# Values of heads 2 and 3 as 512-column products, with their weights split ahead and the first two token tiles run in turns

## The chip, the cores and the metric

The kernel runs on one core of one Trainium2 chip. The metric is the device time of one execution in microseconds (us); the median of several runs counts. Shares and instruction times come from one profiled execution.

## The reference

One layer of an encoder over 1024 tokens of width 1024, all in float32. What matters here is the input projection and the gated linear attention that reads it:

```python
h = rmsnorm(x, norm_mix)
proj = h @ w_in                      # -> q (512), k (512), v (1024), r (1024), decay, pool input, gates
qh, kh: 4 heads of 128 columns       # q scaled by 128 ** -0.5
vh:     4 heads of 256 columns
o = gla_chunked(q, k, v, decay_fwd) + flip(gla_chunked(flipped, decay_bwd))
o = o * rsqrt(mean(o * o)) * gla_norm * silu(r)
```

In `gla_chunked` each chunk of tokens takes scores of q and k, products of the scores with the values, and a state that is carried from chunk to chunk (keys times values, with a decay), forwards and backwards. Then come two branch projections with gates, an output projection, a feed-forward layer and a last norm.

## The kernel before

**Products.** Every float32 operand is split in two float32r parts, high and low (`split_to`: a cast on ACT, a subtraction on DVE or, for most weights, on POOL). A product is three matmuls (`mm3`, L276, through `products` on L274): high x high, high x low, low x high. The normalized and transposed activations lie in `hT`, 8 feature tiles of 128 by 1024 tokens, in SBUF.

**Projections of the heads.** q and k of a head (`project_qk`, L730) are feature-major: for each half of the tokens, 8 steps of `mm3` with 512 columns. Values are token-major: the stationary operand is a tile of 128 tokens, the moving one the weights. For heads 0 and 1 the weights of both heads (512 columns) are kept split in SBUF from the beginning, and `pair_products` (L493) makes both heads' values at once, 512 columns to a matmul. For heads 2 and 3, each in its turn, `values` (L422) makes one token tile: 8 steps of `mm3` with 256 columns, then `split_to` into `vh` and `vl`.

**Weights.** `order` (L238) lists the weight blocks to be loaded; `fetch` issues the next load (`raw` tiles, four buffers, 256 KB each), `prepare` puts the splits of a block in the list `pending`, and `take` hands out the next block and prepares the one after. The split parts lie in `wh` and `wl`, six buffers each. All loads and most stores go through SyncE's queue, in order.

**Order of the work.** Instructions are issued in the order in which the program names them; each engine works through its own in order. `mm3` ends with `pump(columns / 512)` (L161), which counts in steps of one 512-column product: every 2 such steps it runs one entry of `pending`; then, when `pending` is empty, at most one step of `aside` (jobs that form sums of later weights on POOL and store them, `beside` on L677 with `branch_jobs` on L618); then the steps of `side`. A step there is a generator that yields how many units it lets pass. `attention(h, q, k)` (L740) is such a generator: decay terms on ACT and DVE (`exponentials`, `apply_decay`), transposed keys (`kp`, `kt`), then the wait until head h's values are there, the backward states (`kv`, `st`, `sb`, `so`), scores (`sc`, `p`) and the forward pass with outputs (`op`, `o`). Generators run one after another, so head h's attention starts when head h-1's has ended. It runs beside the projections of later heads. `normalize` of a finished head is run by the next head's attention, which also issues the store of its output (`o_out`, `flush`).

**Buffers.** 39 slots of 4 KB a partition hold activations, values, keys, states, sums. PSUM has three banks for projections (`ps_mm`) and five for attention and transposes (`ps_g`). A new tile waits for the last reader of the one that it replaces.

After the heads come eight r products (L1123), beside which head 3's attention ends and the sums of the activations for the next stage are made (`feature_jobs`, L648; tiles `hs`, `trh`, `trl`), and then the gate stage, which multiplies with them.

Of the kernel before, what the change touches and what calls it, by code (L numbers as in the profile page):

```python
# [10 lines left out]
F32 = mybir.dt.float32  # L11
# [6 lines left out]
P = 128  # L18
# [35 lines left out]
def kernel(  # L54
# [38 lines left out]
    def name(s):  # L93
        count[0] += 1
        return f"{s}_{count[0]}"

    def slot(dtype=F32, shape=(2, HALF), s="slot"):
        return slots.tile([P, *shape], dtype, tag="slot", name=name(s))
# [10 lines left out]
    def bank(pool, s="ps"):  # L109
        return pool.tile([P, HALF], F32, tag=pool.name, name=name(s))  # L110

    def as_f32(ap):
        return ap.bitcast(F32)
# [85 lines left out]
    def split_to(hi, lo, src, eng=nc.vector):  # L199
        nc.scalar.copy(hi, src)  # L200
        eng.tensor_tensor(lo, src, as_f32(hi), op=ALU.subtract)  # L201

    def load(src, kts, c0, width):
        per = min(HALF // width, kts)
        tiles = []
        for k0 in range(0, kts, per):
            raw = wts.tile([P, per, width], F32, tag="raw", name=name("raw"), bufs=4)
            nc.sync.dma_start(
                raw[:, :, :],
                src[k0 * P : (k0 + per) * P, c0 : c0 + width].rearrange("(k p) c -> p k c", p=P),  # L210
            )
            tiles.append(raw)
        return tiles

    class Weights:


        def __init__(self, tiles):
            self.per = tiles[0].shape[1]
            self.parts = []  # L220
            self.todo = [partial(self.split, raw) for raw in tiles]
            pending.extend(self.todo)

        def split(self, raw):
            hi = wts.tile(list(raw.shape), F32R, tag="wh", name=name("wh"))[:, :, :]
            lo = wts.tile(list(raw.shape), F32R, tag="wl", name=name("wl"))[:, :, :]
            split_to(hi, lo, raw[:, :, :], nc.gpsimd if hT.tiles else nc.vector)
            self.parts.append((hi, lo))
# [8 lines left out]

    order = []  # L238
    for h in range(HEADS):
        cols_of = [(Q0 + h * DK, DK), (K0 + h * DK, DK), (V0 + h * DV, DV)]  # L240
        order += [(w_in, KT, *c) for c in cols_of[: 2 if h < 2 else 3]]
    order += [(w_in, KT, R0 + j * P, P) for j in range(KT)]
    order = iter(order)
    loaded, ready = [], []
# [6 lines left out]
    def prepare():  # L251
        if not loaded:
            fetch()
        if loaded:
            ready.append(Weights(loaded.pop(0)))

            credit[0] = -2.0

    def take(ahead=True):

        if not ready:
            prepare()
        w = ready.pop(0)
        w.finish()
        if ahead:
            prepare()
        return w
# [3 lines left out]
    def products(ps, a, b, first=True, last=True, onto=False):  # L271

        for n, (i, j) in enumerate(((0, 0), (0, 1), (1, 0))):
            nc.tensor.matmul(ps, a[i], b[j], start=first and n == 0, stop=last and n == 2, skip_group_check=onto)  # L274

    def mm3(ps, a, b, first, last, onto=False):  # L276
        products(ps, a, b, first, last, onto)
        pump(ps.shape[-1] / HALF)
# [15 lines left out]
    def tokens(pair, t):  # L294
        return tuple(p[:, (t % 4) * P : (t % 4 + 1) * P] for p in pair)
# [123 lines left out]
            norm_x(t)  # L419
            yield 2  # L420

    def values(w, v, t):  # L422
        ps = bank(ps_mm)
        for kt in range(KT):
            mm3(ps[:, :DV], tokens(hT(kt, t // 4), t), w(kt), kt == 0, kt == KT - 1)
        split_to(*(part[:, t % 4, :] for part in v[t // 4]), ps[:, :DV])

    lw = [wts.tile([P, 4, 4, 2 * RANK], F32R, tag="wh", name=name("lw")) for _ in range(2)]
    up = slot(F32R, (HEADS, 2, DK), "up")

    def low_rank_weights():
# [3 lines left out]
            nc.vector.tensor_tensor(lw[i][:, :, 3, :], raw, as_f32(lw[i][:, :, 0, :]), op=ALU.subtract)  # L438
        nc.scalar.copy(up[:, :, :, :], uraw[:, :, :, :])
        nc.vector.tensor_tensor(up[32:64], uraw[32:64], as_f32(up[32:64]), op=ALU.subtract)  # L440

    def value_slots():
        return [(slot(F32R, (4, DV), "vh"), slot(F32R, (4, DV), "vl")) for _ in range(2)]

    cols = const.tile([P, 40], F32, tag="cols", name="cols")

# [41 lines left out]
    split_pair_weight()  # L488
    for kp in range(2):
        transpose_tile(trs[kp], xn[1], 1, kp)  # L490
    pair_v = [[], []]

    def pair_products(ts, before=None):  # L493
        banks = [bank(ps_mm) for _ in ts]
        for k in range(KT):
            if before:
                before(k)
            for ps, t in zip(banks, ts):
                mm3(ps[:, :], tokens(hT(k, t // 4), t), pair_w[k], k == 0, k == KT - 1)
        for ps, t in zip(banks, ts):  # L500
            for h in range(2):
                if t // 4 == len(pair_v[h]):
                    pair_v[h].append((slot(F32R, (4, DV), "vh"), slot(F32R, (4, DV), "vl")))
            parts = [[part[:, t % 4, :] for part in v[t // 4]] for v in pair_v]
            halves = [ps[:, h * DV : (h + 1) * DV] for h in range(2)]
            for (hi, _), src in zip(parts, halves):
                nc.scalar.copy(hi, src)
            for (hi, lo), src in zip(parts, halves):
                nc.vector.tensor_tensor(lo, src, as_f32(hi), op=ALU.subtract)

    def first_steps(k):
        if k == 2:
# [204 lines left out]
    def prepare_beside(jobs, every, put=PUT, lag=1):  # L717
        aside.append([beside(chain(*jobs), every, put, lag), every])
# [8 lines left out]
    v_heads, o_heads, unscaled = {}, {}, []  # L727
    HOLD, SCORES = 4.4, 6

    def project_qk():  # L730
        q = slot(s="q")
        k = slot(s="k")
        for dst, scale in ((q, DK**-0.5), (k, 1.0)):
            w = take()
            for half in range(2):
                ps = feature_major(w, hT, half)
                nc.scalar.activation(dst[:, half, :], ps[:, :], AF.Copy, scale=scale)
        return q, k
# [220 lines left out]
    def first_qk():  # L959
        q, k = slot(s="q"), slot(s="k")  # L960
        low_rank(0)
        weights = [take()]
        for half in range(2):
            if half:
                finish_side()
                low_rank(1)
                prepare()
            for n, (dst, scale) in enumerate(((q, DK**-0.5), (k, 1.0))):
                if n == len(weights):
                    weights.append(take(ahead=False))  # L970
                ps = feature_major(weights[n], hT, half)
                nc.scalar.activation(dst[:, half, :], ps[:, :], AF.Copy, scale=scale)
        return q, k

    for h in range(HEADS):
        qk = project_qk() if h else first_qk()
        begin(attention(h, *qk))
        if h == 0:
            for ts in ((7,), (6,), (5, 4)):
                pair_products(ts)  # L980
            v_heads.update(enumerate(pair_v))
            prepare_beside(map(branch_jobs, range(4)), 5)
        if h > 1:
            v = value_slots()
            w = take()
            for t in range(NT):
                values(w, v, t)
            v_heads[h] = v

    class Unit:  # L990

# [1041 lines left out]
```

## Time and profile before

| | |
|---|---|
| time, median of 3 runs (range) | 1379.97 us (1379.44 to 1380.46) |
| the profiled execution | 1380.1 us |
| its span, first to last instruction | 1378.1 us |
| granted TensorE clock, mean | 0.999 |
| instructions | 18207, of them 6514 matmuls |
| value products of heads 2 and 3 | 384 matmuls of 256 columns, 154.3 to 264.5 us |
| head 2's projections begin | about 131 us |
| r products begin | about 269 us |

In the profile PE is TensorE's matmuls, PEld its weight loads, DVE VectorE, ACT ScalarE, POOL GpSimd, SP SyncE. A timeline row has the start and the duration in us, the engine, the line of the kernel and the operation, output and inputs by name; in brackets stands how long the engine was idle before it and what it waited for. A row of the waits has the total in us, how often, and the longest. A row of a stretch of time has its length, then the busy time of an engine in it and the count of instructions, the granted clock, the DMA share and GB/s.

### The profile page before, as it was taken

How to read it: one execution, taken by the hardware profiler on the slowest of the kernel's cores; microseconds unless marked ns; L12 is line 12 of the kernel's file. 1: busy time of each engine (PE TensorE's matmuls, PEld its weight loads, DVE VectorE, ACT ScalarE, POOL GpSimd, SP SyncE). 2: the span in 40 equal slices, each digit the busy share in tenths (PEclk: the TensorE clock that was granted, in tenths of full speed). 3: DMA queues.
4: the chain of work that ended last, by engine and by line, in shares of the span. 5: the costliest groups of instructions: out<-in, count | busy, mean ns of one | idle time of the engine just before them, and what ended most of it. 6: DMA issues, size and time to landing. Idle time of an engine off the chain costs nothing. (4 is left out here: it accounts for less than half of the span.)

```text
span 1378.1 us, 18207 instructions
## 1 busy us (share of the span) xinstructions
PE 1367.6 (99%) x6514; PEld 1147.4 (83%) x6514; DVE 839.8 (61%) x1027; ACT 642.6 (47%) x1170; POOL 750.7 (54%) x554
## 2 busy tenths in 40 slices
PE   9999999999999999999999999999999999999998
PEld 7888899988888888888888888888888888888886
DVE  6364656557745876688883955656656556343375
ACT  7375666655334445554347533333333334444353
POOL 3222617132297646668665276666666667455454
PEclk9999999999999999999999999999999999999999
DMA  6121413312478678996516355555544447985561
GB/s 226 31 62 47 147 62 125 110 48 77 138 230 278 197 229 277 371 394 216 175 61 245 115 176 176 176 176 176 165 143 139 144 136 266 385 306 186 170 214 77
DMA packets 166586, 243.60 MB, mean 177 GB/s; under 512 B 10936, under 2 KB 95968, under 8 KB 166496
## 3 DMA queue, kind: packets, MB, share of 16 engines
q1 hardware_dynamic: 166352, 242.18, 52.3%
q8 instruction: 51, 0.84, 0.3%
q14 instruction: 39, 0.32, 0.1%
q10 hardware_dynamic: 144, 0.26, 0.1%
HBM read 164.55 MB, written 77.86 MB: 176 GB/s over the span
## 5 line engine op out<-in xcount | busy, mean ns | idle before, releaser
L201 POOL TENSOR_TENSOR wl<-fs,wh 128x512 fp32r<-128x512 f32 x120 | 167.6, 1400 | 157.2 <-ACT wh L200 103.2
L274 PE MATMUL ps<-gh,wh 128*128 128x512 f32 x616 | 240.9, 391 | 0.0
L274 PE MATMUL ps<-gl,wh 128*128 128x512 f32 x616 | 240.2, 390 | 0.3 <-DVE gl L1591 0.3
L274 PE MATMUL ps<-gh,wl 128*128 128x512 f32 x616 | 240.0, 390 | 0.0
L201 POOL TENSOR_TENSOR wl<-fraw,wh 128x512 fp32r<-128x512 f32 x90 | 129.7, 1441 | 63.6 <-ACT wh L200 61.2
L274 PE MATMUL ps<-hh,wh 128*128 128x512 f32 x376 | 151.9, 404 | 0.0
L201 POOL TENSOR_TENSOR ol<-gor,oh 128x1024 fp32r<-128x1024 f32 (+1 forms) x42 | 101.7, 2425 | 85.7 <-ACT oh L200 59.6
L274 PE MATMUL ps<-hh,wl 128*128 128x512 f32 x376 | 146.9, 391 | 0.0
L274 PE MATMUL ps<-hl,wh 128*128 128x512 f32 x376 | 146.8, 390 | 0.0
L274 PEld LDWEIGHTS ps<-gl,wh 128*128 128x128 f32 x616 | 115.8, 188 | 24.1 <-DVE gl L1591 0.7
L274 PEld LDWEIGHTS ps<-gh,wh 128*128 128x128 f32 x616 | 115.8, 188 | 24.0 <-ACT hb L1610 0.3
L274 PEld LDWEIGHTS ps<-gh,wl 128*128 128x128 f32 x616 | 115.7, 188 | 24.1
L201 POOL TENSOR_TENSOR wl<-raw,wh 128x512 fp32r<-128x512 f32 x40 | 54.7, 1379 | 121.9 <-ACT wh L200 103.5
L274 PE MATMUL ps<-oh,oh 128*128 128x512 f32 x308 | 120.0, 390 | 0.0
L274 PE MATMUL ps<-oh,ol 128*128 128x512 f32 x308 | 120.0, 390 | 0.0
L274 PE MATMUL ps<-ol,oh 128*128 128x512 f32 x308 | 120.0, 389 | 0.0
L201 POOL TENSOR_TENSOR wl<-wraw,wh 128x512 fp32r<-128x512 f32 x56 | 92.2, 1675 | 44.7 <-ACT wh L200 44.5
L201 DVE TENSOR_TENSOR ol<-wor,oh 128x1024 fp32r<-128x1024 f32 (+1 forms) x42 | 62.8, 1506 | 68.1 <-ACT oh L200 55.5
L200 ACT CAST wh<-fs 128x512 fp32r<-128x512 f32 x120 | 73.8, 615 | 26.1 <-DVE fs L1010 25.1
L274 PEld LDWEIGHTS ps<-hh,wl 128*128 128x128 f32 x376 | 70.6, 188 | 15.0
L274 PEld LDWEIGHTS ps<-hl,wh 128*128 128x128 f32 x376 | 70.9, 188 | 12.9
L274 PEld LDWEIGHTS ps<-hh,wh 128*128 128x128 f32 x376 | 70.8, 188 | 12.8
(279 smaller groups left out, 3126.3 us busy)
## 6 DMA issues: line engine op xcount, KB each, us to landing
fraw<-in_w_ffn_in_dram SPq DMA_DIRECT2D x44, 512.0 KB, 7.2
gor<-g_out SPq DMA_DIRECT2D x35, 512.0 KB, 5.8
g_out<-s SPq DMA_DIRECT2D x44, 256.0 KB, 2.3
raw<-in_w_in_dram SPq DMA_DIRECT2D x40, 256.0 KB, 5.1
fraw<-in_w_in_dram SPq DMA_DIRECT2D x20, 512.0 KB, 7.1
wor<-t_out SPq DMA_DIRECT2D x20, 512.0 KB, 4.5
g_out<-g SPq DMA_DIRECT2D x33, 256.0 KB, 2.5
x<-in_x_dram SPq DMA_DIRECT2D x16, 512.0 KB, 4.5
```

What stands on the lines that cost most here:

```text
L200: nc.scalar.copy(hi, src)
L201: eng.tensor_tensor(lo, src, as_f32(hi), op=ALU.subtract)
L274: nc.tensor.matmul(ps, a[i], b[j], start=first and n == 0, stop=last and n == 2, skip_group_check=onto)
```

## The change

Values of heads 2 and 3 are made together, in the turn of head 2, by a new class `ValueWeights`. Its weights are 8 blocks of 128 features by 512 columns (both heads). It is created as head 2's q weights are taken: two loads at once, four splits put in `pending`, each split first issuing the load four further on. Two more splits are put there when head 2's k weights are taken, and the last two run when the products begin. Feature tiles 6 and 7 are split into slots, the other six into `wh` and `wl`, all six buffers of each. `products` runs token tile 7 with the six weights that come first, then tile 6 with the same six, then tile 7 with the other two, tile 6 with the other two, and tiles 5 to 0 with all eight. Tile 2 issues the load of head 3's q weights; in tile 0, after two weights, their splits are prepared. `keep_values` empties a bank: two casts on ACT, two subtractions on DVE. It is taken out of `pair_products`, which now calls it. The branch sums of `aside` are split in two batches: two jobs after head 0's values with a pace of 3.7 units instead of 5, two after the values of heads 2 and 3 with a pace of 4. `order` no longer has value blocks.

```diff
-        cols_of = [(Q0 + h * DK, DK), (K0 + h * DK, DK), (V0 + h * DV, DV)]
-        order += [(w_in, KT, *c) for c in cols_of[: 2 if h < 2 else 3]]
+        order += [(w_in, KT, c + h * DK, DK) for c in (Q0, K0)]
...
+    class ValueWeights:
+        ORDER = (0, 1, 6, 7, 2, 3, 4, 5)
+        IN_SLOTS = (6, 7)
+        def __init__(self):
+            self.raw, self.parts = [], {}
+            self.load(2)
+            self.splits(4)
+        def load(self, upto):
+            while len(self.raw) < min(upto, KT):
+                k = self.ORDER[len(self.raw)]
+                raw = wts.tile([P, HALF], F32, tag="raw", name=name("raw"), bufs=4)
+                nc.sync.dma_start(raw[:, :], w_in[k * P : (k + 1) * P, V0 + 2 * DV : V0 + 4 * DV])
+                self.raw.append(raw)
+        def split(self):
+            n = len(self.parts)
+            self.load(n + 4)
+            k = self.ORDER[n]
+            if k in self.IN_SLOTS:
+                w = slot(F32R, s="wv")
+                parts = w[:, 0, :], w[:, 1, :]
+            else:
+                parts = [wts.tile([P, HALF], F32R, tag=s, name=name(s))[:, :] for s in ("wh", "wl")]
+            split_to(*parts, self.raw[n][:, :], nc.gpsimd)
+            self.parts[k] = parts
+        def splits(self, n):
+            pending.extend([self.split] * n)
+        def products(self):
+            while pending:
+                pending.pop(0)()
+            vs, banks = ({}, {}), {}
+            self.split()
+            self.split()
+            def steps(t, ks):
+                if t not in banks:
+                    banks[t] = bank(ps_mm)
+                for k in ks:
+                    if (t, k) == (0, 6):
+                        prepare()
+                        credit[0] = 1.0
+                    at = self.ORDER.index(k)
+                    mm3(banks[t][:, :], tokens(hT(k, t // 4), t), self.parts[k], at == 0, at == KT - 1)
+                if ks[-1] == self.ORDER[-1]:
+                    keep_values(vs, t, banks[t])
+            early, late = self.ORDER[:6], self.ORDER[6:]
+            for ks in (early, late):
+                for t in (7, 6):
+                    steps(t, ks)
+            for t in reversed(range(NT - 2)):
+                if t == 2:
+                    fetch()
+                steps(t, self.ORDER)
+            return vs
...
-    def project_qk():
+    def project_qk(last=False):
...
-            w = take()
+            final = last and dst is k
+            w = take(not final)
+            if final:
+                value_weights[0].splits(2)
+            elif last:
+                value_weights.append(ValueWeights())
...
-        qk = project_qk() if h else first_qk()
+        qk = project_qk(h == 2) if h else first_qk()
...
-            prepare_beside(map(branch_jobs, range(4)), 5)
-        if h > 1:
-            v = value_slots()
-            w = take()
-            for t in range(NT):
-                values(w, v, t)
-            v_heads[h] = v
+            prepare_beside(map(branch_jobs, range(2)), 3.7)
+        if h == 2:
+            v_heads.update(zip((2, 3), value_weights.pop().products()))
+            prepare_beside(map(branch_jobs, range(2, 4)), 4)
```

More of the change, by code (lines that the diff above doesn't have):

```diff
@@ L420, in norms @@
             yield 2
[L422 to L426, printed above, removed]
     lw = [wts.tile([P, 4, 4, 2 * RANK], F32R, tag="wh", name=name("lw")) for _ in range(2)]
@@ L440, in low_rank_weights @@
         nc.vector.tensor_tensor(up[32:64], uraw[32:64], as_f32(up[32:64]), op=ALU.subtract)
-    def value_slots():
-        return [(slot(F32R, (4, DV), "vh"), slot(F32R, (4, DV), "vl")) for _ in range(2)]
     cols = const.tile([P, 40], F32, tag="cols", name="cols")
@@ L490, with keep_values @@
         transpose_tile(trs[kp], xn[1], 1, kp)
-    pair_v = [[], []]
+    pair_v = {}, {}
+    def keep_values(vs, t, ps):
+        for v in vs:
+            if t // 4 not in v:
+                v[t // 4] = slot(F32R, (4, DV), "vh"), slot(F32R, (4, DV), "vl")
+        parts = [[part[:, t % 4, :] for part in v[t // 4]] for v in vs]
+        halves = [ps[:, h * DV : (h + 1) * DV] for h in range(2)]
+        for (hi, _), src in zip(parts, halves):
+            nc.scalar.copy(hi, src)
+        for (hi, lo), src in zip(parts, halves):
+            nc.vector.tensor_tensor(lo, src, as_f32(hi), op=ALU.subtract)
     def pair_products(ts, before=None):
@@ L500, in pair_products @@
         for ps, t in zip(banks, ts):
[L501 to L509, printed above, removed]
+            keep_values(pair_v, t, ps)
     def first_steps(k):
@@ L973, in first_qk @@
         return q, k
+    value_weights = []
     for h in range(HEADS):
-        qk = project_qk() if h else first_qk()
+        qk = project_qk(h == 2) if h else first_qk()
         begin(attention(h, *qk))
```

## The prediction

> **What bounds the kernel now.** I read the page first: its head, the engines' busy time, the clock row and the chain of waits.
>
> ```profile
> span 1378.1 us, 18207 instructions
> PE 1367.6 (99%) x6514; PEld 1147.4 (83%) x6514; DVE 839.8 (61%) x1027; ACT 642.6 (47%) x1170; POOL 750.7 (54%) x554
> PEclk9999999999999999999999999999999999999999
> PE 44%; DVE 1%; ACT 1%; issue 0%; POOLq 0%; POOL 0%; DVEq 0%; ACTq 0%
> ```
>
> TensorE is busy 1367.6 of 1378.1 us at an even clock, and nearly all of the chain that can be named is its products on L274. So time can be taken away in two places only: in the pace of the products and in the short holes between them. Busy time is no measure of pace, since matmuls overlap (a 512-column one shows about 390 ns). I read pace from starts. The timeline of TensorE gives it: two rows of the value stage of head 2, and two of head 3's query and key projections.
>
> ```profile
> 171.25 0.28 PE L274 MATMUL ps<-wh,hh 128*128 128x256 f32 x1
> 173.77 0.28 PE L274 MATMUL ps<-wh,hh 128*128 128x256 f32 x1
> 204.40 0.39 PE L274 MATMUL ps<-hh,wh 128*128 128x512 f32 x1
> 215.28 0.39 PE L274 MATMUL ps<-hh,wh 128*128 128x512 f32 x1
> ```
>
> Between the first two lie 21 matmuls without a break: 2.52 / 21 = 0.1200 us for 256 columns. Between the others lie 48: 10.88 / 48 = 0.2267 us for 512. So one step of the kernel's `mm3` (three matmuls) takes 0.360 us at 256 columns and 0.680 at 512. I call the 0.680 us step a unit: it is what the hand-written order of the side work counts in.
>
> Then the holes. The waits of TensorE between 60 and 345 us (all four heads and the first r products):
>
> ```profile
> PE kp L826 <- DVE ke L808: 0.5, 1, 0.5
> PE op L274 <- DVE p L201: 0.4, 2, 0.2
> PE sc L856 <- DVE st L840: 0.2, 1, 0.2
> ```
>
> And TensorE's products (`ps`) in two stretches, head 1's attention and head 2's, each from its first z matmul to its last output:
>
> ```profile
> 131.84:194.16 62.32, 45.63 (x250) 1.00 0.30 93
> 195.06:255.61 60.55, 46.44 (x255) 1.00 0.29 96
> ```
>
> The second stretch holds five products more and is 1.77 us shorter. Five are worth 5 x 0.12 to 5 x 0.227 us, so head 1's attention, which runs beside head 2's values, loses 1.77 + 0.6 to 1.1 = 2.4 to 2.9 us that head 2's doesn't; I take 2.5. The named idle time (1.1 us over all heads) shows less of it.
>
> **The change part by part.**
>
> *Shape.* Heads 2 and 3 each need 8 token tiles x 8 feature tiles x 3 matmuls of 256 columns. The groups by form confirm the count, one of three equal rows:
>
> ```profile
> L274 PE MATMUL ps<-wh,hh 128*128 128x256 f32 x128 | 40.0, 312 | 0.0
> ```
>
> 3 x 128 = 384 go, 192 of 512 columns come: 384 x 0.1200 = 46.08 us against 192 x 0.2267 = 43.52, so -2.56 us, all on TensorE's path. This is the surest term: both paces are measured in this very stage. Against it stands a rule of the Trainium skill, "TensorE: Matmul & The Clock Gate", Part 1, on the measured gap: back-to-back matmuls cost columns over 2.4 GHz plus about 2.5 ns each. By that, 192 fewer matmuls would save 0.48 us; the rows say 2 x 120.0 - 226.7 = 13.3 ns for each, and the measurement decides.
>
> *Evictions, loads, splits.* Each 512-column bank is emptied by two casts on ACT and two subtractions on DVE of 256 columns, as two 256-column banks were:
>
> ```profile
> L200 ACT CAST vh<-ps x16: 349/376/423, 163.2 to 268.1; 128x256 fp32r<-128x256 f32 x16
> L201 DVE TENSOR_TENSOR vl<-ps,vh x16: 414/425/426, 163.6 to 268.5; 128x256 fp32r<-128x256 f32 x16
> ```
>
> The turns hold two of the three banks of `ps_mm`; the third takes tile 5. Tile 7's bank is empty 2 x 0.38 + 2 x 0.43 = 1.6 us after its last step, and is wanted again only after tile 6's two steps and tile 5's eight (6.8 us): hidden; without that cover it would cost TensorE the 1.6 us. Loads: 8 of 256 KB before, 8 now; splits: 8 and 8. They change in place, not in number.
>
> *Where the loads move.* This is the second term. Head 1's lateness comes from the load of head 2's values. ACT, SyncE's queue and DVE there:
>
> ```profile
> 147.88 0.62 ACT L200 CAST wh<-raw 128x512 fp32r<-128x512 f32 x1 [4.14 <-DMA raw<-in_w_in_dram]
> 148.52 1.28 ACT L798 ACT_TABLE_LOAD   x1
> 149.82 0.60 ACT L798 ACTIVATE qe<-z 128x512 f32<-128x512 f32 x1
> ...
> 138.90 2.42 SPq L570 DMA_DIRECT2D o_out<-o  x2
> 141.91 2.73 SPq L208 DMA_DIRECT2D raw<-in_w_in_dram  x4
> ...
> 143.86 0.43 DVE L789 TENSOR_TENSOR z<-z,tot 128x256 f32<-128x256 f32 x1
> ```
>
> SyncE holds the four raw loads behind `o_out` (head 0's output, not normalized yet) until 141.91; ACT runs into the cast at 143.74 and stands 4.14 us. Behind it wait head 1's decay exponentials, whose input is ready at 144.29 but which start at 149.82. Everything after is late: keys, the transposes (0.5 us of PE idle), the state chain, which then holds PSUM banks and delays scores and outputs.
>
> With the change the first two value loads are issued as head 2's q weights are taken, ahead of that `o_out`. But only four raw buffers exist: load n+4 waits for the POOL subtraction of split n, then for a landing.
>
> ```profile
> raw<-in_w_in_dram SPq DMA_DIRECT2D x40, 256.0 KB, 5.1
> ...
> 151.61 1.29 POOL L201 TENSOR_TENSOR wl<-raw,wh 128x512 fp32r<-128x512 f32 x1 [1.74 <-ACT wh L200]
> 152.85 2.20 POOL L809 TENSOR_TENSOR qe<-qe,q 128x512 f32<-128x512 f32 x1
> 157.64 1.32 POOL L706 TENSOR_TENSOR wsum<-wsum 128x512 f32<-128x512 f32 x1
> 162.50 1.28 POOL L809 TENSOR_TENSOR qe<-qe,q 128x512 f32<-128x512 f32 x1
> ```
>
> Following ACT's order with these prices: the first split is done at about 141, so its successor's load is issued at 142 and lands at 147; the exponentials of the first run start at about 149 instead of 149.82. The sixth split (load issued at 145.5, landed at 151) stands in front of the second run's, about 0.5 us ahead of before. So the wait shrinks, it does not vanish. But the slack grows too: the second transpose now falls behind a whole unit (154.98) and not a half, and its key should be ready at about 154.4. The chain of states, one per 1.46 us, starts about 3.0 us after its first product, not 3.64:
>
> ```profile
> 157.58 0.28 PE L274 MATMUL kv<-vh,kt 128*128 128x256 f32 x1
> 161.22 0.47 DVE L838 TENSOR_SCALAR st<-kv,fac 128x256 f32<-128x256 f32 x1
> 165.36 0.48 DVE L840 SCALAR_TENSOR_TENSOR st<-kv,fac,so 128x256 f32<-128x256 f32 x1 [0.98 <-ACT so L848]
> 166.82 0.48 DVE L840 SCALAR_TENSOR_TENSOR st<-kv,fac,so 128x256 f32<-128x256 f32 x1 [0.98 <-ACT so L848]
> ```
>
> Counting the five banks of `ps_g` along this chain, each state product and the score block then find a free bank within about 0.2 us. I take 2.0 of the 2.5 us back. Bounds: none (0), if the loads land later than I think, to all 2.5; head 3's wait for p (one of the two in the waits above) may go too, 0.2 us named.
>
> *The turns.* Six of the eight weights are there when the values begin; the last two need the buffers that the last key product frees. On ACT their two casts (0.62 us each) stand ahead of the next transposed keys, on POOL their subtractions stand ahead of the last `qe`; the chain of states waits for those keys, but DVE, with a scan of 1.74 us and three smaller steps of the last decay in front of them, is later anyway. Cover on TensorE: 2 x 6 units = 8.2 us, and 7 state products of 0.36 us, and a score block:
>
> ```profile
> 158.31 1.74 DVE L778 TENSOR_TENSOR_SCAN z<-carry,la 128x512 f32<-128x512 bf16 x1
> 154.30 0.28 PE L274 MATMUL ps<-wh,hh 128*128 128x256 f32 x1
> 230.35 1.95 PE L856 MATMUL sc<-qe,ke 128*128 128x128 f32 x16
> ```
>
> 8.2 + 2.5 + 1.95 is 12.6 us after 154.3, the start of the values, so the seventh weight is needed near 166.9. POOL has, from the fourth value split (about 148), eleven subtractions and multiplications (three of them `qe`, four branch sums) until the eighth weight: 11 x 1.29 = 14.2, so 162. Hidden by more than 4 us; its price if the cover is gone stands with the rivals. At the other end, head 3's q weights are split when the last tile has used its first two weights: 0.62 + 1.29 us against six units, 4.1 us, hidden.
>
> *Heads 2 and 3.* The yields of `attention` add up to 34.8 units before it needs values and 59 in all. In units from head 0's attention, head 1's runs from 64 to 123 and head 2's from 123; the values of head 2 now come with head 3's at 96 + 64 = 160, where 123 + 34.8 = 158 are wanted. Head 3's attention can begin when its projections are done, at 192, 10 units after head 2's ended before (182). The sums for the next stage so begin one half of an r product later, 8 units or 5.4 us. What is late next is the gate stage, which reads them:
>
> ```profile
> 368.11 1.23 DVE L691 TENSOR_TENSOR trl<-hs,trh 128x1024 fp32r<-128x1024 f32 x1 [0.45 <-ACT trh L700]
> ...
> 382.23 0.39 PE L274 MATMUL ps<-trh,wh 128*128 128x512 f32 x1
> ```
>
> The last is ready 12.9 us before the first is used: hidden. Half of the branch sums move behind the values, one POOL step of 1.32 us in 4 units (2.7 us), which leaves POOL room for the two splits of every 16 units; without that room a split would come up to 1.3 us late, of 4 units of lead. For all I can't see (39 buffers that I count full once, beside the outputs of head 1; a store that a buffer waits for) I add 0.3 us, between 0 and 3.
>
> *Sum.* 1380.1 (the profiled run: span 1378.1 and 2.0 around it; the median of 1379.97 is 0.13 below) - 2.56 - 2.0 + 0.3 = 1375.8 us.
>
> **The rivals.** A measurement of this kernel tells about 0.2%, 2.8 us, from no change.
>
> *Only the shape counts.* The wait for raw loads comes back at the fifth or sixth split and head 1 loses its 2.5 us as before, or heads 2 and 3 lose as much in new places. For it: four buffers make each load hang on POOL. Against: the first loads no longer stand behind `o_out`. 1380.1 - 2.56 + 0 to 1 = 1377.5 to 1378.5, about 1378, within 0.2%. Chance 0.20.
>
> *POOL becomes the bound in the turns: slower.* The eleven POOL steps before the eighth weight stretch when DVE works beside them: `qe` took 2.20 us at 152.85 and 1.28 at 162.50. The Trainium skill, "GPSIMD Engine Reference", specification table, says that its SBUF interfaces are shared with VectorE; the trace agrees with these two numbers. The cover ends at an average of (166.9 - 148) / 11 = 1.72 us a step; each 0.1 us above costs TensorE 1.1 us. To eat the gain of 4.3 and 2.8 more the average must be 1.72 + 7.1 / 11 = 2.37 us, worse than the worst row, or a load must land some 7 us late behind a store as at 141.91. Both in part give 1383 to 1386, say 1384. Chance 0.10.
>
> *The change does less than it says.* If a matmul cost nothing but its columns, dropping 192 would bring nothing, and without another gain the time would be 1380.1, within 0.2%. Both paces, measured in the stage itself, speak against it; 512-column products among state products would have to run slower than the rows show. Chance 0.02. The page's 2.5 ns each would make it 1379.6.
>
> **How the numbers follow.** The forecast, 1375.8 with 1374 to 1377.2 of its own, has 0.68. Its low end takes head 1's loss at its upper bound of 2.9, head 3's 0.2 and no unseen cost (1380.1 - 2.56 - 2.9 - 0.2 = 1374.4), and 0.4 for the spread of runs: 1374.0. Up, the range takes in the first and third rival and the 3 us of unseen cost on the shape alone (1380.1 - 2.56 + 3 = 1380.5). So 1374.0 to 1380.5, leaving the slower case and a little below. Faster 0.68; within 0.2% 0.20 + 0.02 = 0.22; slower 0.10.
>
> **What the profile after would show.** Right: no 128x256 `ps` group from L274, 192 more 128x512 ones at 0.227 us from start to start; the 4.14 us on `wh` from DMA gone or below 2; no `kp` on `ke` wait; the first trh product 4 us earlier. Wrong: TensorE waiting for POOL `wl` near 166.9, ACT on raw for more than 3 us between 140 and 152, or heads 2 and 3 with waits of their own.

## The result, and the profile after

The change made the kernel slower by 0.2%: 1382.41 us (1381.07 to 1383.37, 16 runs) against 1379.55 (1379.02 to 1380.46, 16 runs), a ratio of 1.0020 with a 95% interval of 1.0013 to 1.0028. The prediction was 1375.8 with 1374.0 to 1380.5, so the result lies 1.9 us outside its range, on the other side of no change.

The first profiled execution of the changed kernel took 1381.07 us, the least of its runs. A second one took 1382.33 us, as most runs did; unless said otherwise the rows of the changed kernel are of this second profile. The head of its page, the busy time of the engines, the clock, and the chain of waits:

```profile
span 1380.5 us, 17839 instructions
PE 1365.6 (99%) x6322; PEld 1134.8 (82%) x6322; DVE 838.3 (61%) x1027; ACT 642.4 (47%) x1170; POOL 747.8 (54%) x554
PEclk9999999999999999999999999999999999999999
PE 44%; DVE 1%; ACT 1%; issue 0%; POOLq 0%; POOL 0%; DVEq 0%; ACTq 0%
```

TensorE has 192 matmuls less (6514 to 6322) and is 2.0 us less busy, but the span is 2.4 us longer: it now stands for longer. Where, the waits of TensorE between 60 and 345 us say. In these rows stand the waiting group, what it waited for, the total in us, how often and the longest:

```profile
PE op L979 <- ACT sf L901: 2.1, 2, 1.7
PE kp L883 <- DVE ke L865: 0.9, 1, 0.9
PE op L273 <- DVE p L201: 0.7, 3, 0.2
PE op L273 <- ACT p L200: 0.4, 1, 0.4
PE ps L273 <- POOL wl L201: 0.3, 1, 0.3
PE kv L273 <- DVE kt L201: 0.3, 1, 0.3
```

Before, this list held 1.1 us in three rows; now it holds 4.7 in six.

The heads can be compared by stretches that both kernels have: from the first z matmul of one head to that of the next, and from head 3's z to the first product with `trh`, with which the gate stage begins. First the kernel before, then the changed one (TensorE alone; length, busy time, instructions, clock, DMA share, GB/s):

```profile
131.84:195.06 63.22, 62.19 (x402) 1.00 0.30 92
195.06:256.50 61.44, 61.44 (x406) 1.00 0.29 95
256.50:382.23 125.73, 125.45 (x668) 1.00 0.33 104
```

```profile
131.84:195.07 63.23, 61.39 (x322) 1.00 0.21 67
195.07:264.63 69.56, 69.04 (x358) 1.00 0.28 84
264.63:384.70 120.07, 117.77 (x604) 1.00 0.36 117
```

The first stretch, where head 1's attention runs, is as long as before to 0.01 us, though its value products are fewer. (In the first profile it was 62.02 us; the first experiment shows why.) Heads 2 and 3, whose work is divided otherwise now, take 69.56 + 120.07 = 189.63 us together where they took 187.17. So all of the loss, 2.46 us, arises there, and all that was to be won is missing in both. Everything behind lasts as long as it did: 1378.1 - 382.23 = 995.9 us before, 1380.5 - 384.70 = 995.8 after.

### The profile page after: what moved, and what is told of

Same layout as the page of the kernel before. It is cut to its first block, busy times and chain, and to the rows that moved or that the text cites. A ratio compares the mean times of both kernels' runs of the same rounds, so it can differ in the third digit from the quotient of the medians.

```text
span 1379.2 us, 17839 instructions
## 1 busy us (share of the span) xinstructions
PE 1366.3 (99%) x6322; PEld 1135.7 (82%) x6322; DVE 836.6 (61%) x1027; ACT 642.4 (47%) x1170; POOL 750.6 (54%) x554
## 5 line engine op out<-in xcount | busy, mean ns | idle before, releaser
L201 POOL TENSOR_TENSOR wl<-raw,wh 128x512 fp32r<-128x512 f32 x38 | 51.3, 1361 | 125.6 <-ACT wh L200 99.8
```

## The experiments

Each kernel's time is the median of its runs; "the changed kernel" stands for 1382.4 us. Kernels of one group ran on the same chip, each group on another; the kernel before had 1379.40 to 1379.55 us on all four, so that a comparison across groups is uncertain by some 0.15 us more.

### First group: the changed kernel again, and three edits

**The changed kernel again.**

> The changed kernel once more, for a second profile: the median (1382.4 us) lies 1.3 us above the profiled run (1381.07), whose TensorE waits explain only +1.1 us against before. Theory A (fixed waits): the new waits seen in the first profile (outputs on sf 1.7 and 0.5, weights of head 3's q 0.3) come again with the same size, and what is left is spread over DMA landings: one more wait of about 1 us, on weights or activations, that the first profile lacks. Theory B (pace): no new wait, but products a little slower throughout (0.1% would be 1.3 us). Time 1382 to 1383 by both.

1382.40 us (1381.45 to 1382.77), ratio 1.0020 (1.0010 to 1.0029). Its trace and that of the first profile agree within 0.15 us up to 152 us. Then the repeated one falls 1.3 us behind and stays so. VectorE and POOL, first profile, then second:

```profile
152.34 1.23 DVE L835 TENSOR_TENSOR_SCAN z<-carry,la 128x512 f32<-128x512 bf16 x1
152.41 3.60 POOL L696 TENSOR_TENSOR wsum<-wsum,wsum 128x512 f32<-128x512 f32 x2
```

```profile
152.48 2.40 DVE L835 TENSOR_TENSOR_SCAN z<-carry,la 128x512 f32<-128x512 bf16 x1
152.49 3.46 POOL L696 TENSOR_TENSOR wsum<-wsum,wsum 128x512 f32<-128x512 f32 x2
156.19 0.66 PE L883 MATMUL kp<-ident,ke 128*128 128x128 f32 x4 [0.87 <-DVE ke L865]
```

Where the scan came first it takes 1.23 us, and the two POOL sums, of 1.29 us each alone, take 3.60 with the wait. In the second profile scan and POOL sum begin within 0.01 us of each other, and the scan takes 2.40, 1.2 us more; a transpose then waits for the key that depends on it. That the POOL sum went first there, and the second sum then waited for the scan, is read from the lengths (1.29 and 1.23 make 2.5), as the starts don't tell. Less than a tenth of a microsecond decides which it is.

**One r product more held back.** `BY`, the number of r products whose gates are put off until head 3's attention is over, goes from 3 to 4.

```diff
-    BY = 3
+    BY = 4
```

> The changed kernel with gates on r from the fifth r product on (BY 4, not 3), so that no gate step of r stands before the end of head 3's attention. If head 3's later attention meets the first Silu on ACT, as the 1.67 us wait on sf in the first profile suggests: that wait goes, 1.6 to 2.0 us less than the changed kernel, about 1380.5. Rival (the loss is elsewhere, the wait only hides a later one): within 0.5 us of the changed kernel.

1384.55 us (1383.21 to 1386.31), 2.1 more than the changed kernel: the expectation fell. The wait of 1.7 us for `sf` is gone from its list, but a transpose now waits 1.2 us for a gated product (`o`), and the first `trh` product begins only 0.6 us sooner, at 384.09 instead of 384.70. The last of the late gates run on ACT until 383.8, right ahead of the gate stage's own casts, and there TensorE loses more than was saved:

```profile
388.86 0.50 PE L273 MATMUL ps<-trh,wh 128*128 128x512 f32 x1 [1.85 <-ACT ga L1436]
```

**The shape undone.** Each 512-column product of the change as two of 256 columns into the two halves of its bank; turns, loads, splits and evictions stay. In this run the second half's first matmul starts its bank anew, so that the first half's sums lack their first terms.

```diff
-                    mm3(banks[t][:, :], tokens(hT(k, t // 4), t), self.parts[k], at == 0, at == KT - 1)
+                    for j in range(2):
+                        c = slice(j * DV, (j + 1) * DV)
+                        products(banks[t][:, c], tokens(hT(k, t // 4), t), tuple(w[:, c] for w in self.parts[k]), ...)
+                    pump(1)
```

> The changed kernel with each 512-column product of values of heads 2 and 3 made as two of 256 columns in the two halves of the same bank; order, weights and side work as in the change. If the shape is worth what the starts said (13.3 ns for each of 192 matmuls): 2.6 us more than the changed kernel, about 1385. Rival (512-column products gain nothing here, the loss is what it is without them): no more than 0.7 us above it.

1382.68 us (1382.40 to 1383.14), only 0.3 more than the changed kernel. The surest term of the prediction, 2.56 us, is hardly there in the time. Why is the subject of the third and fourth group.

**The sums alone.** The kernel before, with the branch sums in the two batches that the change makes, and nothing else.

```diff
-            prepare_beside(map(branch_jobs, range(4)), 5)
+            prepare_beside(map(branch_jobs, range(2)), 3.7)
...
+            if h == 2:
+                prepare_beside(map(branch_jobs, range(2, 4)), 4)
```

> The kernel before with only the branch sums in two batches as in the change (two jobs at a pace of 3.7, two at 4 after head 2's values). If the moved sums cost something by themselves (POOL or stores in the way): 0.5 to 2 us slower than before. Else within 0.3 us of 1379.6.

1386.95 us (1385.12 to 1387.22), 7.4 us over the kernel before. SyncE's queue and ACT show the path of the first loss (a second, 2.1 us, is a wait of outputs for `p` that ends at 241.5):

```profile
144.72 16.52 SPq L687 DMA_DIRECT2D s_out<-wsum  x4
161.34 2.10 SPq L208 DMA_DIRECT2D raw<-in_w_in_dram  x4
...
165.36 0.62 ACT L200 CAST wh<-raw 128x512 fp32r<-128x512 f32 x1 [2.84 <-DMA raw<-in_w_in_dram]
```

The sums stood in POOL's queue behind other work, their stores behind them held SyncE until 161, and the raw loads of head 3's weights, issued at 149.90 before, came behind those stores. ACT stood 2.84 us in front of the cast that needed them, with a cast of values queued behind it; VectorE's next state stood behind the subtraction that belongs to that cast, and TensorE waited 2.4 us for the state. The two waits are 4.5 of the 7.4 us. Most of the rest is the clock: behind each of them the granted clock of TensorE falls to about half, 0.52 from 167.15 to 170.42 and 0.50 from 242.49 to 245.34, and products of 256 columns start 0.21 us apart there, not 0.12. At half pace these 3.27 and 2.85 us hold some 1.5 us too much each, by my estimate. The one run of the four that kept a mean clock of 0.999 took 1385.12, the others, with 0.996 and 0.997, 1386.8 to 1387.2. So the pace and place of the sums are no free choice. The changed kernel has its value loads ahead of these stores and does not show this wait.

### Second group: three losses, each mended alone, and together

**The gate held half a product longer.** As with `BY` = 4, but only the first half of r product 3 is put off.

```diff
-        if j < BY:
+        if j <= BY:
             whole_r = slot(s="r")
...
-            if j < BY:
+            if (j, half) <= (BY, 0):
                 nc.scalar.copy(whole_r[:, half, :], ps[:, :])
```

> The gate of the first half of r product 3 (its Silu with the table load, its transposes and its multiplication) is held back until head 3's attention is over, as those of products 0 to 2 are; all else is the changed kernel. Theory A (head 3's attention now ends 32 units later against the r products and meets this gate; the 1.67 us wait for sf at 326 and the 0.57 us stretch around it are this collision): the wait for sf goes, nothing takes its place, 1.7 to 2.7 us less than the changed kernel, 1379.7 to 1380.7. Rival (the side work is only moved, as with four whole products held, where DVE and ACT came late to the first gate products instead): the sf wait goes but the gate stage waits for ga or o, and the time stays within 0.7 us of 1382.4 or rises to 1384.

1380.55 us (1379.52 to 1381.04): theory A. What it removed, in the changed kernel, on TensorE, ACT and VectorE:

```profile
327.39 0.70 PE L979 MATMUL op<-sf,qe 128*128 128x256 f32 x2 [1.67 <-ACT sf L901]
...
323.04 1.28 ACT L1152 ACT_TABLE_LOAD   x1
324.33 0.63 ACT L1152 ACTIVATE sr<-r 128x512 f32<-128x512 f32 x1
...
325.00 1.41 DVE L1162 SCALAR_TENSOR_TENSOR o<-tp,cols,sr 128x512 f32<-128x512 f32 x2 [2.98 <-ACT sr L1152]
326.32 0.47 DVE L897 SCALAR_TENSOR_TENSOR st<-kv,fac,so 128x256 f32<-128x256 f32 x1
326.83 0.51 ACT L901 ACTIVATE sf<-st,fac 128x256 f32<-128x256 f32 x1 [1.39 <-DVE st L897]
```

Head 3's last state (`st`) stands on VectorE behind two gate multiplications, which wait for the Silus, which wait for a table load on ACT; TensorE waits for the scaled copy of that state (`sf`). With the half product held, the same places read:

```profile
323.33 0.48 DVE L897 SCALAR_TENSOR_TENSOR st<-kv,fac,so 128x256 f32<-128x256 f32 x1 [1.44 <-ACT op L981]
326.19 1.28 ACT L1152 ACT_TABLE_LOAD   x1
```

The state comes first, the table load after the last output, and the stretch of head 3 is 118.15 us instead of 120.07. The gate stage shows no new wait.

**The sums moved off the scans.** The second job of the first batch of sums comes five empty steps later (`idle(5)` yields them).

```diff
-            prepare_beside(map(branch_jobs, range(2)), 3.7)
+            prepare_beside([branch_jobs(0), idle(5), branch_jobs(1)], 3.7)
```

> Four of the branch sums on POOL are moved about 12 us later, past head 1's scans; all else is the changed kernel. Theory B (VectorE's scan and POOL's two-input operations shut each other out: the scan at 152.48 took 2.40 us beside a POOL sum that began with it, 1.23 us where it came first): the scan there takes 1.23 to 1.4 us in every run, the key's transpose waits under 0.2 us for ke instead of 0.87, and the time is 0.8 to 1.4 us less, 1381.0 to 1381.6. Rival (the 1.3 us between the two profiles of the changed kernel is noise of another place): scan still over 2 us or no wait gone, time within 0.4 us of 1382.4.

1381.53 us (1381.15 to 1383.44), 0.9 less. The scan takes its 1.23 us, no `kp` waits for `ke`, and head 1's stretch is 62.24 us. One run of the ten was at 1383.44; what that one met is not known.

```profile
152.51 1.23 DVE L839 TENSOR_TENSOR_SCAN z<-carry,la 128x512 f32<-128x512 bf16 x1
```

**The sixth split behind the exponentials.**

```diff
-                value_weights[0].splits(2)
+                value_weights[0].splits(1)
...
                 nc.scalar.activation(dst[:, half, :], ps[:, :], AF.Copy, scale=scale)
+                if final and half == 0:
+                    value_weights[0].split()
```

> The sixth value split, which stood in front of head 1's decay exponentials on ACT and waited 1.8 to 2.2 us there for its load, is called behind the first run's exponentials; all else is the changed kernel. Theory C (this one split is why head 1's 2.5 us did not come back): exponentials start at 147.3 to 148.0 instead of 149.9, the wait of the transposes for ke goes, head 1's stretch from its first z to head 2's (63.2 us in the repeated profile) shrinks by 1.0 to 2.0 us, time 1380.4 to 1381.4. Rival (the stretch is set by what comes behind: scans, keys, states one per 1.46 us, PSUM banks): exponentials start early, yet the stretch shrinks by under 0.5 us and the time stays over 1381.9.

1380.61 us (1380.09 to 1381.63): theory C. ACT in the changed kernel, then with the edit:

```profile
148.11 0.62 ACT L200 CAST wh<-raw 128x512 fp32r<-128x512 f32 x1 [1.82 <-DMA raw<-in_w_in_dram]
148.75 1.28 ACT L855 ACT_TABLE_LOAD   x1
150.04 0.60 ACT L855 ACTIVATE qe<-z 128x512 f32<-128x512 f32 x1
```

```profile
145.32 0.62 ACT L200 CAST wh<-raw 128x512 fp32r<-128x512 f32 x1
145.96 1.28 ACT L857 ACT_TABLE_LOAD   x1
147.26 0.60 ACT L857 ACTIVATE qe<-z 128x512 f32<-128x512 f32 x1
```

The exponentials start 2.8 us sooner and head 1's stretch is 1.8 us shorter, 61.40 us, though the later split costs a new wait of 0.5 us for `wl`. The scan still ran beside work on POOL, but now it came first (1.32 us), so that this edit takes in most of what the one before mends.

**Together**, with the splits of head 3's first weights one unit sooner (`credit[0]` set to 2.0).

> The three edits together, and the splits of head 3's first weights begun one unit sooner (for the 0.46 us wait for wl at 225 to 228). If the three losses are independent, as theories A to C have it: 2.0 + 1.1 + 1.2 + 0.4, less what B and C share (the same transposes, about 1), so 3.3 to 4.3 us less than the changed kernel: 1378.1 to 1379.1, as fast as the kernel before or up to 1.4 us faster. Rival (each mended wait only uncovers the next on the chain of states): under 2 us less, over 1380.4.

1378.65 us (1377.92 to 1379.03), 3.75 less than the changed kernel, ratio to the kernel before 0.9993 (0.9984 to 1.0003). The three add up as expected, 4.5 us less what the last two share. The earlier credit did nothing: the wait for `wl` at 225 is still 0.46 us.

### Third group: what the shape is worth, two more waits, and the kernel before mended

**The mended kernel with the shape undone** (the edit of the first group, each bank started by its first half alone).

> The mended kernel with each 512-column value product made as two of 256 columns, the turns and all else as they are: the shape term with the large waits out of the way. 192 matmuls more. Theory D (the shape is worth its 13.3 ns for each matmul wherever TensorE doesn't wait; in the changed kernel the waits behind it gave it back): 1.8 to 2.6 us over the mended kernel's 1378.65, so 1380.4 to 1381.3. Rival (beside the states it is worth less than 2.56, as each period of a state product and a value unit was 2.270 us with 512 columns and 2.295 with 256, and what waits remain take the rest): 0.2 to 1.2 us, under 1379.9.

1378.98 us (1378.06 to 1379.70), 0.3 over the mended kernel (0.5, if each is taken against the kernel before on its own chip): the rival. The same steps of TensorE in the mended kernel, and in that with the halves:

```profile
196.50 0.39 PE L812 MATMUL z<-lrT,up 128*128 128x512 f32 x1
213.73 0.60 PE L889 MATMUL kp<-ident,ke 128*128 128x128 f32 x4
224.05 0.28 PE L273 MATMUL kv<-vl,kt 128*128 128x256 f32 x1
225.38 0.50 PE L273 MATMUL ps<-hh,wl 128*128 128x512 f32 x1 [0.46 <-POOL wl L201]
226.55 0.28 PE L273 MATMUL kv<-vl,kt 128*128 128x256 f32 x1
239.85 0.28 PE L273 MATMUL op<-vl,p 128*128 128x256 f32 x1
```

```profile
196.53 0.39 PE L818 MATMUL z<-lrT,up 128*128 128x512 f32 x1
214.76 0.60 PE L895 MATMUL kp<-ident,ke 128*128 128x128 f32 x4
225.34 0.28 PE L273 MATMUL kv<-vl,kt 128*128 128x256 f32 x1
227.08 0.28 PE L273 MATMUL kv<-vl,kt 128*128 128x256 f32 x1
239.75 0.28 PE L273 MATMUL op<-vl,p 128*128 128x256 f32 x1
```

From z to `kp` only value products run, and nothing is waited for: 17.23 us against 18.23, with 25 value steps between, which have 75 matmuls more in halves; 1.00 / 75 = 13.3 ns each, the price of the prediction. The lead of the wide products grows to 1.29 us. Then the wait for `wl`, which the halves don't have, takes it down to 0.53, and at 239.85 it is -0.10: some 0.15 us went at the score block, most of the rest at the products that wait for `p`. TensorE came sooner to points that ACT, POOL and VectorE reach when they do.

**Both waits taken away.** Head 3's first weights are split at once when their buffers are free, two units after the last tile begins; each value bank is emptied 1.2 units later, behind the state that is due.

```diff
-                        credit[0] = 2.0
+                        while pending:
+                            pending.pop(0)()
...
-                    keep_values(vs, t, banks[t])
+                    soon(1.2, partial(keep_values, vs, t, banks[t]))
```

> The mended kernel with both splits of head 3's first weights called at once when their buffers are free (two units after the last tile begins) and each value bank emptied 1.2 units after its last product, behind the state that is due. Theory E: the wait for wl at 225 (0.46 named, 0.63 with the pipe) and that for sf at 192 (0.46, 0.62) go: 0.8 to 1.3 us less than the mended kernel, 1377.3 to 1377.9. Rival (the evictions or casts land on another due step): within 0.4 us of 1378.65, or above it.

1376.04 us (1375.58 to 1376.77), ratio 0.9973 (0.9962 to 0.9984). Theory E by its sign, but 2.6 us and not 0.8 to 1.3: the waits of outputs for `p` fell from three to two as well. In the profiles head 1's stretch went from 61.21 to 60.17 us and head 2's from 69.66 to 68.57, while head 3's grew by 0.6; why the gain is larger than the waits named was not traced.

**The kernel before, with its value splits one unit later.**

```diff
-    def project_qk():
+    def project_qk(hold=0.0):
...
+            if scale == 1.0:
+                credit[0] -= hold
...
-        qk = project_qk() if h else first_qk()
+        qk = project_qk(1.0 * (h == 2)) if h else first_qk()
```

> The kernel before, with the splits of head 2's value weights begun one unit later, so that the first run's decay exponentials stand ahead of the first of them on ACT; nothing else. It asks whose gain the late split is. Theory F (head 1's 2.5 us were the exponentials behind the load, in both kernels): head 1's stretch from z to z falls from 63.2 us by 1.0 to 2.0, time 1377.6 to 1378.6. Rival (in the kernel before the other runs' exponentials still stand behind three casts, and the stretch keeps its loss): over 1379.0.

1377.46 us (1377.11 to 1377.96), ratio 0.9984 (0.9975 to 0.9994): theory F, a little more than expected. Head 1's stretch:

```profile
131.69:192.40 60.71, 60.71 (x403) 1.00 0.30 96
```

63.22 us have become 60.71: the 2.5 us by which the prediction held head 1 to be late were there to be had in the kernel before too, by one number and without the change (1.9 us by the medians on that chip).

### Fourth group: the shape with fewer waits, and the turns

**The second mended kernel again.**

> The second mended kernel unchanged, so that the one below has it on its own chip: 1375.6 to 1376.5.

1376.30 us (1375.67 to 1376.90), ratio 0.9975 (0.9966 to 0.9985). Its waits of TensorE between 60 and 345 us, all that is left of the 4.7 us:

```profile
PE op L273 <- DVE p L201: 0.4, 2, 0.2
PE op L273 <- ACT p L200: 0.4, 1, 0.4
```

**The same with the shape undone.**

> The second mended kernel with its value products as two of 256 columns each. Theory D2 (the shape's gain was taken back by waits for wl and p that are due at a fixed time whatever TensorE's pace; the wait for wl is gone now, those for p are not): 0.8 to 1.6 us over the second mended kernel, 1376.8 to 1377.7. If all cover were gone it would be 2.56. Rival (the rest of the gain is taken back as well): under 0.5 us over it.

1377.69 us (1377.32 to 1378.50), 1.4 over it: theory D2. With the wait for `wl` gone, the shape is worth 1.4 us instead of 0.3. This pair also shows where the other 1.2 us of the 2.56 stay. Neither profile names a wait of TensorE between the first value product and the first product of head 3's projections, and this stretch takes 64.43 us (154.16 to 218.59) with 512 columns and 66.53 (154.20 to 220.73) with 256: 2.10 us, not 2.56. Among states and outputs the gain for each matmul is smaller than between value products: four periods of head 1's forward pass (179.11 to 188.17, and 179.74 to 188.88), each with one value unit, take 9.06 and 9.14 us, so 0.02 us for three matmuls, 6.7 ns each. The remaining 0.7 us are lost between that stretch and the gate stage. The waits for `p` stand there, but only 0.2 us more of them are named with the wide products, so that the 0.7 are not fully accounted for.

**The changed kernel without its turns**, the tiles 7 to 0 in order, each with all eight weights.

```diff
-            early, late = self.ORDER[:6], self.ORDER[6:]
-            for ks in (early, late):
-                for t in (7, 6):
-                    steps(t, ks)
-            for t in reversed(range(NT - 2)):
+            for t in reversed(range(NT)):
```

> The changed kernel with the value tiles in plain order, 7 to 0, each with all eight weights: no turns. Of the repeated profile, the seventh step of tile 7 would begin at about 162.8 and the last two weights are ready on POOL at 163.7 and 164.9: TensorE waits some 1.4 us there. If the turns hide what the prediction said: 1.0 to 2.5 us over the changed kernel's 1382.4, 1383.4 to 1384.9. Rival (the wait takes the place of later ones on the chain of states): within 0.6 us of 1382.4.

1384.52 us (1383.29 to 1385.78), 2.1 more than with them. TensorE waits longer than expected, and later waits become shorter (that for `ke` is gone). Behind the wait the clock falls here too: two products of 512 columns start 0.43 us apart, not 0.23, and the granted clock is 0.50 from 164.52 to 167.72: by the same estimate 1.6 us more. The runs with a mean clock of 0.999 and 1.000 took 1383.3 to 1384.0, those with 0.997 and 0.998 1385.1 to 1385.8.

```profile
163.78 0.50 PE L273 MATMUL ps<-wl,hh 128*128 128x512 f32 x1 [3.39 <-POOL wl L201]
...
164.94 0.63 PE L273 MATMUL ps<-wh,hh 128*128 128x512 f32 x1
165.37 0.63 PE L273 MATMUL ps<-wl,hh 128*128 128x512 f32 x1
```

## Why the prediction was wrong, step by step

**What bounds the kernel: right.** In both kernels the clock is even and the products are nearly all of the chain; the differences that were traced are holes on TensorE, the number of its matmuls, and in two experiments the clock behind a long hole.

**Shape, -2.56: right in pace, mis-sized as a term.** 13.3 ns for each matmul dropped held where value products follow one another. Among states and outputs it was about half of that, and over a stretch without named waits 2.10 us came of the 2.56: the prediction's own condition for its third rival, that 512-column products among state products run slower than its rows, was met in part. And the whole product was put "on TensorE's path", as if nothing stood behind it. In the changed kernel undoing it cost 0.3 us, in the mended one 0.3, in the second mended one 1.4. The prediction's third rival, a matmul that costs nothing but its columns, would look the same by the time alone; the pace between z and `kp` tells them apart. The 0.48 us that followed from the rule of the Trainium skill, "TensorE: Matmul & The Clock Gate", Part 1, lies nearer to the first two times, but not for its reason.

**Head 1, -2.0: the step failed; the bound of 0 was the truth.** The prediction saw that the sixth split would stand in front of exponentials and put the loss at "about 0.5 us ahead of before" for the second run's. In fact it stood in front of the first run's, with a load that landed at 148.1, and the exponentials started at 150.04 where they had started at 149.82. The runs that call splits later show what this order costs: in the kernel before all of the 2.5 us (60.71). In the changed kernel the stretch fell to 61.40, but a part of that is the scan: with only the sums moved it was 62.24, with both edits (and the gate held) 61.21, so that the order by itself is worth about 1.0 there and the scan about as much. The second transpose's wait was forecast to go; it was there in four of the five profiles with the turns, these sums and this order of splits, because the scan in front of its key met POOL's sums. The prediction had named the contention, by the specification table of the Trainium skill's page "GPSIMD Engine Reference", but applied it to POOL's steps and not to VectorE's scan.

**Turns, 0: right.** The last two weights were ready before they were wanted, and without the turns 2.1 us are lost. The rival of POOL as the bound in the turns did not happen. It was the only one that forecast a slower kernel; that the kernel did become slower has other causes, and is no point in its favour.

**Evictions and head 3's weights, 0: wrong by small sums.** Two casts of values on ACT and their subtractions on VectorE stood in front of the last state of head 1 (0.47 us), and the cast of head 3's second weight stood on ACT behind exponentials of head 2 whose input came late (0.30): the prediction compared its 0.62 + 1.29 us with the cover of 4.1, and not the queue in front of it. The second of these, like the 1.67 us for `sf`, is one of the "waits of their own" in heads 2 and 3, the third of its signs of error.

**Heads 2 and 3, a shift that is hidden: the step that gave the wrong sign.** The prediction named one reader of head 3's attention, the sums for the gate stage, and found 12.9 us of room. By its own units the other reader can be seen: head 3's projections end at 192, its attention has 59 more, so it ends at 251; the first half of r product 3, whose gate is not put off, ends at 192 + 48 + 8 = 248. Before, it ended at 182 + 59 = 241, 7 units ahead of that gate; the shift of 10 units, which the prediction had, carried it past. (The 32 units of the expectation above don't follow from these counts.) The traces agree: in the kernel before, whose r products begin at 264.6 and not at about 269, the last output came at 317.35, before the second half of r product 2 was copied out (318.88), and in the changed kernel at 327.39, after the Silus that come with that gate had begun (324.33). Holding that gate gave back 1.85 us.

The balance: the forecast was 1375.8 us. Of the 6.6 us to 1382.4, 3.75 came back when the gate, the sums and the sixth split were moved, and 2.3 to 2.6 more with the two small waits; the second mended kernel, 1376.0 and 1376.3, is where the prediction stood. Part of its gain is not the change's: the kernel before with one number altered has 1377.46. Between the two lie 1.4 us, on the same chip: that is what the change was worth once its neighbours stood right. So the forecast number was reached in the end, but not by the sum that gave it. Undoing the shape cost as much in the fourth group; that it is the same 1.4 us was not shown.

## What to carry to other kernels

A gain on the engine that sets the time is worth only as much as lies between it and the next point where that engine waits for another; look for that point before the gain is written down in full. When side work is moved against the main line, list every reader and every neighbour on each queue at the new place, by position: the one forgotten here was three units away and cost 1.9 us. And where an engine works strictly in order, a cast that waits for a load belongs behind the work whose inputs are there.

## What the hardware showed that was not expected

By these traces VectorE's scan and POOL's two-input operations shut each other out, as far as for the length of a whole instruction. The scan took 1.23 us when it came first or alone and 2.40 when a POOL sum began within 0.01 us of it; where the scan won, POOL's pair took 3.60 instead of 2 x 1.29. The Trainium skill, "SBUF — State Buffer", section "SBUF: two separate sides", says that whichever of the two starts first keeps the shared port pair for its whole instruction, VectorE's operations with two inputs in SBUF among them; the scan reads `carry` and `la` there, and these numbers agree. So two executions of one kernel that differ by 0.1 us at that place differ by 1.3 us at the end. A change of 7.4 us came from nothing but the pace and place of sums on POOL, through stores that held SyncE's queue for 16.5 us.

In these traces a wait of TensorE of 2 us or more cost more than its length. Behind the waits of 2.09, 2.44 and 3.39 us the granted clock fell to about 0.5 for some 3 us; behind those of 1.67 and 1.85 us it stayed at 1.00. Where between them the clock begins to fall, and whether the length of the wait alone decides it, was not tried.
